# MLP down projection, segments 0 to 2: seven block products of sums for each pair of column tiles

## Chip, cores and metric

The kernel runs on one core of a Trainium2 chip. The metric is the device time of one execution in microseconds (us), the median of several runs. The profile is of one further execution.

## What is computed

A decoder trunk of two layers runs on 512 prompt positions and 64 sample positions, T = 576 columns together. Layer 0 mixes with attention and an S5 scan, layer 1 with a Mamba-2 SSD. After each mixer stands an MLP of width 4096 on a model width of 1024, and this is what the change touches:

```python
def _sq_relu_mlp(h, w_up, w_down):
    a = jax.nn.relu(h @ w_up)
    return (a * a) @ w_down
...
x = x + _rmsnorm(m, p['norm_mix_post'][i])
h = _rmsnorm(x, p['norm_mlp_pre'][i])
x = x + _rmsnorm(_sq_relu_mlp(h, p['w_mlp_up'][i], p['w_mlp_down'][i]), p['norm_mlp_post'][i])
```

All is float32. Each operand of a large product is split into a high and a low part (fp32r), and three matmuls, high by high, high by low and low by high, take the place of one.

## The kernel before

Activations lie transposed: features on the 128 partitions, the 576 columns in two halves of 288 (`hf` 0 and 1). A weight block `w` is 1024 input features by 128 output features, one DMA of 512 KB. `split_block` makes its parts `wh` (ScalarE copy, line 289) and `wl` (VectorE subtraction, line 304), each 128x1024 values, in a ring of NS = 9 buffers; the raw block has a ring of NW = 2.

`project3` goes over (tile, half) in the order of `rounds`. One such group is eight chunks of three matmuls (lines 318, 339, 340) of 128x128 by 288 columns, 24 in all, summed in one of three PSUM banks `mm`, and then read by the function `evac`. With `first` or `last` given to `rounds`, all tiles pass for half 0 and then all for half 1, so that all eight weight blocks must be held; out_proj_even and the last down projection do so (TAIL = 8), and so does the first up projection of a layer (LEAD = 8).

`mlp` runs four segments. In each, eight up tiles (16 groups) give 1024 of the 4096 hidden features: `up` takes relu times the norm's factor on VectorE (line 991), the square on ScalarE (line 286), and splits the result into `a2` (line 289 on ScalarE, line 347 on VectorE). Then the down projection (16 groups) multiplies this segment's eight chunks with `w_dn`; `down` copies the sums to `m` in segment 0 (ScalarE, line 289) and adds them to `m` in segments 1 to 3 (VectorE, line 1005). In segment 3 it also gathers the squares for the norm that follows (line 203 on GpSimd). So the down projections of segments 0 to 2 in two layers are 6 stages of 16 groups of 24 matmuls.

The order of instructions on every engine is that of a scheduler which plays the program through with estimated durations; each engine then works strictly in its order and waits on semaphores. Tiles of a ring wait until the earlier tile in the same buffer is no longer read. The SSD part (lines 1369, 1389) and the odd layer's out_proj (line 1198) are not touched by the change; their rows serve for durations.

Of the kernel before, what the change touches and what calls it, by code (L numbers as in the profile page):

```python
# [9 lines left out]
F32 = mybir.dt.float32  # L10
F32R = mybir.dt.float32r
ACTF = mybir.ActivationFunctionType
ALU = mybir.AluOpType
# [6 lines left out]
T = SEQ + TS  # L20
HALF = T // 2
HV = ((0, HALF), (HALF, T))
# [195 lines left out]
class _Kernel:  # L218
    def __init__(self, tc, a, ctx):
# [5 lines left out]
        self.n = self.blocks = self.turn = 0  # L225
        self.share = SHARE_EVEN
        self.groups, self.pins, self.last = 0, [], None


    def nm(self, s):  # L230
# [58 lines left out]
        return self.nc.scalar.activation(out, in_, ACTF.Identity, **kw)  # L289


    def split_block(self, src, ring=None, cuts=1):

        raw = self.block(src, (8, 128), ring, cuts)
        pool, bufs = self.wp
        hi = pool.tile([128, 8, 128], F32R, tag="wh", name=self.nm("wh"), bufs=bufs)
        lo = pool.tile([128, 8, 128], F32R, tag="wl", name=self.nm("wl"), bufs=bufs)
        self.blocks += 1
        eng = self.nc.gpsimd if self.share and self.blocks % self.share == 0 else self.nc.vector
        n = 8 // cuts  # L300
        for i in range(cuts):
            f = lambda t: t[:, i * n:i * n + n].rearrange("p a b -> p (a b)")
# [673 lines left out]

    def mlp(self, layer, h, r, mx, done):

        m = self.halves(self.mring)
        nc = self.nc  # L980
        sums = [_Squares(self, 8, SQ_M[hf]) for hf in range(2)]
        up_w, dn_w = self.a[f"w_up{layer}"], self.a[f"w_dn{layer}"]
        for seg in range(4):
            a2 = {}

            def up(i, hf, ps):
                sl = slice(*HV[hf])
                if hf == 0:
                    a2[i] = [mx.tile([128, T], F32R, tag="a2" + p, name=self.nm("a2"), bufs=NA2) for p in "hl"]
                t = mx.tile([128, HALF], F32, tag="a2t", name=self.nm("a2t"), bufs=3)  # L990
                nc.vector.scalar_tensor_tensor(t, ps, 0.0, r[hf], op0=ALU.max, op1=ALU.mult)  # L991
                self.act(t, t, ACTF.Square)
                self.split_into(a2[i][0][:, sl], a2[i][1][:, sl], t)

            first = 8 * seg
            mts = list(range(first, first + 8))
            self.share = 0 if seg else SHARE_LEAD
            self.project3(lambda i: up_w[i, 0], self.rounds(mts, first=0 if seg else LEAD), self.chunk(h), up)

            def down(i, hf, ps):  # L1000
                out = m[hf][:, i, :]
                if seg == 0:
                    self.copy_a(out, ps)
                else:
                    nc.vector.tensor_tensor(out, out, ps, ALU.add)  # L1005
                if seg == 3:
                    sums[hf].add(out)
                    if i == 7:
                        done(hf, m[hf], sums[hf])

            self.project3(lambda i: dn_w[i, seg], self.rounds(range(8), last=TAIL if seg == 3 else 0), lambda c, hf: [t[:, slice(*HV[hf])] for t in a2[first + c]], down)


    def odd(self, h, spill, done):
# [416 lines left out]
    def run(self):  # L1431
        nc, tc, a = self.nc, self.tc, self.a
        self.start()
        o = self.even()
# [39 lines left out]

        def mlp_pools(es):
            mx = es.enter_context(tc.tile_pool(name=self.nm("mx"), bufs=1, reuse_waits="tile"))
            self.wp = es.enter_context(tc.tile_pool(name=self.nm("mw"), bufs=1, reuse_waits="tile")), NS
            return mx

        h2 = []  # L1480
        with ExitStack() as es:
            mx = mlp_pools(es)
            self.ln_exp_table()
            self.out_proj_even(o, to_mlp(0))
            self.mlp(0, h, r, mx, to_odd)
        self.odd(h2, xd, to_mlp(1, (None, self.xring)))
# [20 lines left out]
SQ_X = ("p", "p")  # L1507
SQ_P = ("pv", "pv")
SQ_G = "pv"
NS = 9  # L1510
NSE = 2
NSO = 2
NHB = 4
# [20 lines left out]
PS_D = "t"  # L1534
GLU_Q = 1
PS_Y = "at"
NA2 = 9
TAIL = 8
NCV = 6
NT2 = 5  # L1540
# [42 lines left out]
```

## Time and profile before

| what | value |
|---|---|
| median of 3 runs | 1802.25 us (1798.43 to 1804.58) |
| profiled execution | 1804.89 us |
| its span, first to last instruction | 1803.1 us |
| mean granted TensorE clock | 0.961 |
| TensorE matmul busy | 1707.7 us (95%) |
| VectorE, ScalarE, GpSimd busy | 1010.7, 695.8, 401.9 us |

Busy shares are means over stages that differ. The two MLPs lie at about 390 to 800 us and 1380 to 1790 us; up and down stages take turns in them, some 51 us each. Matmuls overlap in the array, so a single one shows about 295 ns while one starts every 133 ns. A line number can be that of a helper that many callers use; the names of the tiles tell them apart. In the profile `project` is the PSUM bank of `project3`, `a` the split activations of `mlp`, `a2t` their unsplit form.

### The profile page before, as it was taken

The page shows a single profiled execution, that of the slowest core. Times are in us where ns is not written, and L with a number is a line of the kernel's source. Part 1 is how long each engine was busy: PE and PEld are TensorE (multiplying, and loading weights), DVE is VectorE, ACT ScalarE, POOL GpSimd, SP SyncE. Part 2 cuts the span into 40 slices and gives each one's busy share as a digit, 9 for nine tenths or more (in the row PEclk, how much of TensorE's full clock was granted, in tenths as well). Part 3 has the DMA queues.
Part 4 walks back from the last instruction along what each step waited for, and adds up shares of the span by engine and source line. Part 5 has one row for each costly group of instructions (what it writes and reads, how often), then busy time and mean ns, then how long its engine had stood idle before and what let it go on. Part 6 is the DMA issues. An engine that isn't in the chain of part 4 may idle for free. (4 is left out here: it accounts for less than half of the span.)

```text
span 1803.1 us, 31677 instructions
## 1 busy us (share of the span) xinstructions
PE 1707.7 (95%) x13007; PEld 1575.2 (87%) x13007; DVE 1010.7 (56%) x1789; ACT 695.8 (39%) x1306; POOL 401.9 (22%) x489
## 2 busy tenths in 40 slices
PE   9998999899999999998899899999977999999997
PEld 8975666799999999997789789898767999999997
DVE  8755435476243433357788757877768624343334
ACT  5233434465242322334325536335245524132331
POOL 3532100141000000134465434432343100000002
PEclk9998889899999999998799999999968999999999
DMA  8568553522222222222132141232513322222201
GB/s 279 100 241 288 190 198 140 170 94 94 83 82 83 83 84 87 77 66 85 47 132 85 48 163 55 96 129 73 174 40 125 109 87 85 83 83 83 83 24 53
DMA packets 81649, 197.41 MB, mean 109 GB/s; under 512 B 20352, under 2 KB 32000, under 8 KB 81504
## 3 DMA queue, kind: packets, MB, share of 16 engines
q1 hardware_dynamic: 57568, 174.72, 28.2%
q10 hardware_dynamic: 23936, 20.67, 3.9%
q8 instruction: 102, 1.67, 0.4%
q14 instruction: 43, 0.35, 0.1%
HBM read 176.92 MB, written 18.44 MB: 108 GB/s over the span
## 5 line engine op out<-in xcount | busy, mean ns | idle before, releaser
L318 PE MATMUL project<-h,wh 128*128 128x288 f32 x1808 | 547.0, 304 | 15.9 <-ACT raw L289 7.9
L339 PE MATMUL project<-h,wh 128*128 128x288 f32 x1808 | 546.4, 303 | 6.8 <-DVE h L395 6.5
L340 PE MATMUL project<-h,wl 128*128 128x288 f32 x1808 | 544.8, 302 | 2.5 <-DVE wl L304 2.5
L289 ACT ACTIVATE wh<-w 128x1024 fp32r<-128x1024 f32 (+1 forms) x215 | 225.4, 1050 | 458.0 <-PE project L339 347.7
L318 PEld LDWEIGHTS project<-h,wh 128*128 128x128 f32 x1808 | 348.1, 193 | 26.2 <-ACT raw L289 9.2
L339 PEld LDWEIGHTS project<-h,wh 128*128 128x128 f32 x1808 | 348.7, 193 | 15.8 <-DVE h L395 9.0
L340 PEld LDWEIGHTS project<-h,wl 128*128 128x128 f32 x1808 | 348.3, 193 | 9.2 <-issue 4.5
L304 DVE TENSOR_TENSOR wl<-w,wh 128x1024 fp32r<-128x1024 f32 (+1 forms) x196 | 243.9, 1247 | 188.9 <-ACT wh L289 187.3
L340 PE MATMUL project<-a,wl 128*128 128x288 f32 x1024 | 302.1, 295 | 0.0
L318 PE MATMUL project<-a,wh 128*128 128x288 f32 x1024 | 301.6, 295 | 0.0
L339 PE MATMUL project<-a,wh 128*128 128x288 f32 x1024 | 301.5, 294 | 0.0
L318 PEld LDWEIGHTS project<-a,wh 128*128 128x128 f32 x1024 | 192.1, 188 | 0.2
L340 PEld LDWEIGHTS project<-a,wl 128*128 128x128 f32 x1024 | 192.1, 188 | 0.1
L339 PEld LDWEIGHTS project<-a,wh 128*128 128x128 f32 x1024 | 192.1, 188 | 0.1
L203 POOL TENSOR_TENSOR nacc<-nacc,nsq 128x288 f32<-128x288 f32 x88 | 82.8, 942 | 485.9 <-ACT nsq L286 457.8
L1005 DVE TENSOR_TENSOR m<-m,project 128x288 f32<-128x288 f32 x96 | 43.5, 453 | 173.7 <-PE project L340 173.7
L304 POOL TENSOR_TENSOR wl<-w,wh 128x1024 fp32r<-128x1024 f32 x19 | 46.1, 2426 | 398.3 <-ACT wh L289 390.1
L991 DVE SCALAR_TENSOR_TENSOR a2t<-project,nht 128x288 f32<-128x288 f32 x128 | 58.2, 457 | 104.6 <-PE project L340 104.6
L286 ACT ACTIVATE a2t<-a2t 128x288 f32<-128x288 f32 x128 | 55.6, 435 | 113.5 <-DVE a2t L991 113.4
L347 DVE TENSOR_TENSOR a<-a2t,a 128x288 fp32r<-128x288 f32 x128 | 61.8, 486 | 53.7 <-ACT a L289 53.7
L1191 PE MATMUL out_proj<-x,wh 128*128 128x288 f32 x256 | 77.3, 304 | 3.0 <-DVE m L1198 2.6
L1045 DVE SCALAR_TENSOR_TENSOR cacc<-raw,cw,cacc 128x600 f32<-128x600 f32 x72 | 69.7, 968 | 14.1 <-POOL cacc L1043 13.1
(481 smaller groups left out, 2671.7 us busy)
## 6 DMA issues: line engine op xcount, KB each, us to landing
w<-in_w_up SPq DMA_DIRECT2D x64, 512.0 KB, 3.5
w<-in_w_dn SPq DMA_DIRECT2D x64, 512.0 KB, 3.5
w<-in_ck SPq DMA_DIRECT2D x40, 512.0 KB, 5.0
w<-in_cv SPq DMA_DIRECT2D x40, 512.0 KB, 6.0
w<-in_w_in_o SPq DMA_DIRECT2D x40, 512.0 KB, 3.5
w<-in_w_out_o SPq DMA_DIRECT2D x20, 512.0 KB, 3.5
hb<-in_h SPq DMA_DIRECT2D x32, 256.0 KB, 4.0
out_ssm_s<-hn ACTq DMA_DIRECT2D x32, 256.0 KB, 3.6
```

The costliest lines, as they stand in the source:

```text
L203: eng.tensor_tensor(self.acc[way], self.acc[way], sq, ALU.add)
L286: return self.nc.scalar.activation(out, in_, func, **kw)
L289: return self.nc.scalar.activation(out, in_, ACTF.Identity, **kw)
L304: eng.tensor_tensor(f(lo), f(raw), f(hi).bitcast(F32), ALU.subtract)
L318: self.nc.tensor.matmul(*args, **kw)
L339: self.nc.tensor.matmul(out, wh[:, c, :], xl, start=False, stop=False)
L340: self.nc.tensor.matmul(out, wl[:, c, :], xh, start=False, stop=(c == 7))
L347: self.nc.vector.tensor_tensor(lo, t, hi.bitcast(F32), ALU.subtract)
L991: nc.vector.scalar_tensor_tensor(t, ps, 0.0, r[hf], op0=ALU.max, op1=ALU.mult)
L1005: nc.vector.tensor_tensor(out, out, ps, ALU.add)
L1045: stt(acc, raw[:, k:k + 600], cw[:, 4 * m + k:4 * m + k + 1], acc, op0=ALU.mult, op1=ALU.add)
L1191: nc.tensor.matmul(out, wh[:, c, :], gh[:, k, :], start=(k == 0), stop=False)
```

## The change

For segments 0 to 2 the down projection takes output tiles in four pairs. In a pair the operands are seen as 2x2 blocks: output tiles by K halves (four blocks of 128 by 512, `a11` to `a22`, from two weight blocks), and K halves by column halves (four blocks of 512 by 288). Seven products of sums of blocks (the Winograd form of Strassen's scheme) take the place of eight products; one product is four chunks of three matmuls, 12 in all.

GpSimd makes the four sums of weight blocks (`s1` to `s4`, 128x512 each) and the sums of activations (`t1` to `t4`, four subtractions of 128x288 for each of four chunks in a segment); each sum is split again. Products go in the order of PAIR_STEPS. Products 1 and 2 share one PSUM sum, 6, 7 and 4 another, 5 and 3 a third: the bank is read after every product and the next product goes on adding to it. Product 1 goes to a new accumulator `e1`, the rest to the tiles of `m`; in the first segment the first reading of each accumulator is a ScalarE copy, all other readings are VectorE additions. In segment 3 GpSimd adds `e1` to the other three tiles of each pair (12 additions of 128x288 a layer). Up tiles run in the order 0, 4, 1, 5, 2, 6, 3, 7 in segments 0 to 2.

Buffers: NS goes from 9 to 5, `a2t` from 3 to 8 buffers (NC), the activation parts have one buffer each; where eight weight blocks must be held, the buffers of `t2` to `t4` serve as three more (`spare`).

```diff
--- before.py
+++ after.py
@@ -225,6 +225,7 @@
         self.n = self.blocks = self.turn = 0
         self.share = SHARE_EVEN
         self.groups, self.pins, self.last = 0, [], None
+        self.mx, self.spare = None, []
     def nm(self, s):
@@ -289,12 +290,19 @@
         return self.nc.scalar.activation(out, in_, ACTF.Identity, **kw)
+    def part_tiles(self):
+        if self.spare:
+            k = self.spare.pop(0)
+            return [self.mx.tile([128, 4 * HALF], F32R, tag=f"at{k}{p}", name=self.nm("w" + p), bufs=1)[:, :1024]
+                    .rearrange("p (a b) -> p a b", a=8) for p in "hl"]
+        pool, bufs = self.wp
+        return [pool.tile([128, 8, 128], F32R, tag="w" + p, name=self.nm("w" + p), bufs=bufs) for p in "hl"]
     def split_block(self, src, ring=None, cuts=1):
         raw = self.block(src, (8, 128), ring, cuts)
-        pool, bufs = self.wp
-        hi = pool.tile([128, 8, 128], F32R, tag="wh", name=self.nm("wh"), bufs=bufs)
-        lo = pool.tile([128, 8, 128], F32R, tag="wl", name=self.nm("wl"), bufs=bufs)
+        hi, lo = self.part_tiles()
         self.blocks += 1
         eng = self.nc.gpsimd if self.share and self.blocks % self.share == 0 else self.nc.vector
         n = 8 // cuts
@@ -976,39 +984,129 @@
     def mlp(self, layer, h, r, mx, done):
         m = self.halves(self.mring)
         nc = self.nc
         sums = [_Squares(self, 8, SQ_M[hf]) for hf in range(2)]
         up_w, dn_w = self.a[f"w_up{layer}"], self.a[f"w_dn{layer}"]
+        e1 = [mx.tile([128, HALF], F32, tag=f"e1{i}", name=self.nm("e1"), bufs=1) for i in range(4)]
         for seg in range(4):
-            a2 = {}
+            last = seg == 3
+            act = {k: [mx.tile([128, 4 * HALF], F32R, tag=f"a{k}{p}", name=self.nm(f"a{k}"), bufs=1)
+                       .rearrange("p (a b) -> p a b", a=4) for p in "hl"]
+                   for k in (("11", "21", "22", "t1") if last else ("11", "21", "22", "t1", "t2", "t3", "t4"))}
+            names = {(0, 0): "11", (1, 0): "21", (0, 1): "t1", (1, 1): "22"}
+            keep = {}
             def up(i, hf, ps):
-                sl = slice(*HV[hf])
-                if hf == 0:
-                    a2[i] = [mx.tile([128, T], F32R, tag="a2" + p, name=self.nm("a2"), bufs=NA2) for p in "hl"]
-                t = mx.tile([128, HALF], F32, tag="a2t", name=self.nm("a2t"), bufs=3)
+                kh, j = divmod(i % 8, 4)
+                t = m[0][:, i, :] if seg == 0 and hf == 0 else mx.tile([128, HALF], F32, tag="a2t", name=self.nm("a2t"), bufs=NC)
                 nc.vector.scalar_tensor_tensor(t, ps, 0.0, r[hf], op0=ALU.max, op1=ALU.mult)
                 self.act(t, t, ACTF.Square)
-                self.split_into(a2[i][0][:, sl], a2[i][1][:, sl], t)
-            first = 8 * seg
-            mts = list(range(first, first + 8))
+                keep[kh, hf, j] = t
+                part = lambda k: [p[:, j, :] for p in act[k]]
+                if last or (kh, hf) != (0, 1):
+                    self.split_into(*part(names[kh, hf]), t)
+                if not last and hf == 1:
+                    sub = lambda o, a, b: nc.gpsimd.tensor_tensor(o, a, b, ALU.subtract)
+                    if kh == 0:
+                        t1 = keep["t1", j] = mx.tile([128, HALF], F32, tag="a2t", name=self.nm("a2t"), bufs=NC)
+                        sub(t1, t, keep[0, 0, j])
+                        self.split_into(*part("t1"), t1)
+                    else:
+                        t1, b12, b21 = keep["t1", j], keep[0, 1, j], keep[1, 0, j]
+                        sub(t1, t, t1)
+                        self.split_into(*part("t2"), t1)
+                        sub(b12, t, b12)
+                        self.split_into(*part("t3"), b12)
+                        sub(b21, b21, t1)
+                        self.split_into(*part("t4"), b21)
+            mts = [8 * seg + i for i in ((0, 4, 1, 5, 2, 6, 3, 7) if not last else range(8))]
             self.share = 0 if seg else SHARE_LEAD
+            if seg == 0:
+                self.spare = [2, 3, 4]
             self.project3(lambda i: up_w[i, 0], self.rounds(mts, first=0 if seg else LEAD), self.chunk(h), up)
+            if not last:
+                self.down_pairs(lambda i: dn_w[i, seg], act, m, e1, seg == 0, mx)
+                continue
+            self.spare = [2, 3, 4]
+            for i in range(4):
+                for o in (m[0][:, 2 * i + 1, :], m[1][:, 2 * i, :], m[1][:, 2 * i + 1, :]):
+                    nc.gpsimd.tensor_tensor(o, o, e1[i], ALU.add)
             def down(i, hf, ps):
                 out = m[hf][:, i, :]
-                if seg == 0:
-                    self.copy_a(out, ps)
-                else:
-                    nc.vector.tensor_tensor(out, out, ps, ALU.add)
-                if seg == 3:
-                    sums[hf].add(out)
-                    if i == 7:
-                        done(hf, m[hf], sums[hf])
-            self.project3(lambda i: dn_w[i, seg], self.rounds(range(8), last=TAIL if seg == 3 else 0), lambda c, hf: [t[:, slice(*HV[hf])] for t in a2[first + c]], down)
+                nc.vector.tensor_tensor(out, out, ps, ALU.add)
+                sums[hf].add(out)
+                if i == 7:
+                    done(hf, m[hf], sums[hf])
+            self.project3(lambda i: dn_w[i, seg], self.rounds(range(8), last=TAIL),
+                          lambda c, hf: [p[:, c % 4, :] for p in act[names[c // 4, hf]]], down)
+    def pair_parts(self, src, i, mx):
+        nc = self.nc
+        raw = self.block(src(2 * i), (8, 128)), self.block(src(2 * i + 1), (8, 128), (mx, "w2", 2))
+        flat = lambda t, a: t[:, 4 * a:4 * a + 4, :].rearrange("p a b -> p (a b)")
+        a11, a12, a21, a22 = [flat(w, a) for w in raw for a in range(2)]
+        sums = [mx.tile([128, 8, 128], F32, tag="ws", name=self.nm("ws"), bufs=2) for _ in range(2)]
+        s1, s2, s4, s3 = [flat(w, a) for w in sums for a in range(2)]
+        out = {}
+        def split(key, pieces):
+            hi, lo = self.part_tiles()
+            for a, (k, t) in enumerate(zip(key, pieces)):
+                self.copy_a(flat(hi, a), t)
+                nc.vector.tensor_tensor(flat(lo, a), t, flat(hi, a).bitcast(F32), ALU.subtract)
+                out[k] = lambda c, hi=hi, lo=lo, a=a: (hi[:, 4 * a + c, :], lo[:, 4 * a + c, :])
+        op = lambda o, a, b, f: nc.gpsimd.tensor_tensor(o, a, b, f)
+        op(s1, a21, a22, ALU.add)
+        op(s2, s1, a11, ALU.subtract)
+        split((1, 2), (a11, a12))
+        split((5, 6), (s1, s2))
+        op(s4, a12, s2, ALU.subtract)
+        op(s3, a11, a21, ALU.subtract)
+        split((3, 7), (s4, s3))
+        split((4,), (a22,))
+        return out
+    def down_pairs(self, src, act, m, e1, first, mx):
+        nc = self.nc
+        right = {1: "11", 2: "21", 3: "22", 4: "t4", 5: "t1", 6: "t2", 7: "t3"}
+        bank_of = {1: "a", 2: "a", 6: "b", 7: "b", 4: "b", 5: "c", 3: "c"}
+        begin = 1, 6, 5
+        parts, banks, seen = {}, {}, set()
+        for i, p in PAIR_STEPS:
+            if i not in parts:
+                parts[i] = self.pair_parts(src, i, mx)
+            kind = bank_of[p]
+            if p in begin:
+                banks[i, kind] = (self.dacps if i % 2 else self.accps)("pair") if kind == "b" else self.mmps("pair")
+            ps = banks[i, kind][:, :HALF]
+            for c in range(4):
+                wh, wl = parts[i][p](c)
+                xh, xl = [t[:, c, :] for t in act[right[p]]]
+                go_on = dict(start=False, skip_group_check=p not in begin)
+                nc.tensor.matmul(ps, wh, xh, **(dict(start=True) if p in begin and c == 0 else go_on), stop=False)
+                nc.tensor.matmul(ps, wh, xl, **go_on, stop=False)
+                nc.tensor.matmul(ps, wl, xh, **go_on, stop=c == 3)
+            m11, m21, m12, m22 = [m[hf][:, 2 * i + k, :] for hf in range(2) for k in range(2)]
+            name, out = {1: (0, e1[i]), 2: (11, m11), 6: (12, m12), 7: (22, m22), 4: (21, m21), 5: (22, m22), 3: (12, m12)}[p]
+            if first and (i, name) not in seen:
+                seen.add((i, name))
+                self.copy_a(out, ps)
+            else:
+                nc.vector.tensor_tensor(out, out, ps, ALU.add)
     def odd(self, h, spill, done):
@@ -1474,6 +1572,7 @@
         def mlp_pools(es):
             mx = es.enter_context(tc.tile_pool(name=self.nm("mx"), bufs=1, reuse_waits="tile"))
+            self.mx = mx
             self.wp = es.enter_context(tc.tile_pool(name=self.nm("mw"), bufs=1, reuse_waits="tile")), NS
             return mx
@@ -1481,6 +1580,7 @@
         with ExitStack() as es:
             mx = mlp_pools(es)
             self.ln_exp_table()
+            self.spare = [2, 3, 4]
             self.out_proj_even(o, to_mlp(0))
             self.mlp(0, h, r, mx, to_odd)
         self.odd(h2, xd, to_mlp(1, (None, self.xring)))
@@ -1507,7 +1607,7 @@
 SQ_X = ("p", "p")
 SQ_P = ("pv", "pv")
 SQ_G = "pv"
-NS = 9
+NS = 5
 NSE = 2
 NSO = 2
 NHB = 4
@@ -1534,7 +1634,11 @@
 PS_D = "t"
 GLU_Q = 1
 PS_Y = "at"
-NA2 = 9
+NC = 8
+PAIR_STEPS = [(0, 1), (0, 5), (0, 2), (0, 6), (0, 3), (0, 7)]
+for _i in range(1, 4):
+    PAIR_STEPS += [(_i, 1), (_i - 1, 4)] if _i == 1 else [(_i, 1)]
+    PAIR_STEPS += [(_i, _p) for _p in (6, 2, 7, 5, 4, 3)]
 TAIL = 8
 NCV = 6
 NT2 = 5
```

## Rows read from the trace of the kernel before

**Rows 1.** The page, part 1: engine, busy time (share of the span), instructions.

```profile
PE 1707.7 (95%) x13007; PEld 1575.2 (87%) x13007; DVE 1010.7 (56%) x1789; ACT 695.8 (39%) x1306; POOL 401.9 (22%) x489
```

**Rows 2.** Busy time by stretch; columns as in the first line.

```profile
core 0: us, PE busy (x) PEld busy (x) DVE busy (x) ACT busy (x) POOL busy (x), PEclk, DMA share, GB/s
...
446.10:497.20 51.10, 51.10 (x388) 51.10 (x387) 9.91 (x9) 14.15 (x24) 0.00 (x0) 1.00 0.25 84
497.20:548.30 51.10, 51.10 (x385) 51.10 (x385) 23.66 (x41) 21.82 (x40) 0.00 (x0) 1.00 0.24 83
548.30:599.40 51.10, 51.10 (x388) 51.10 (x387) 17.30 (x25) 8.48 (x8) 0.00 (x0) 1.00 0.24 84
...
341.00:391.00 50.00, 47.34 (x327) 46.31 (x327) 29.52 (x35) 29.37 (x57) 17.24 (x17) 0.93 0.35 117
1340.00:1410.00 70.00, 57.91 (x375) 55.01 (x374) 56.17 (x86) 40.64 (x81) 33.68 (x32) 0.88 0.33 113
```

**Rows 3.** Timeline of TensorE in a down stage: start us, duration us, line.

```profile
659.56 0.29 PE L340 MATMUL project<-a,wl 128*128 128x288 f32 x1
659.69 0.29 PE L318 MATMUL project<-a,wh 128*128 128x288 f32 x1
659.82 0.29 PE L339 MATMUL project<-a,wh 128*128 128x288 f32 x1
```

**Rows 4.** Timeline of VectorE there; idle before and releaser in brackets.

```profile
656.73 0.46 DVE L1005 TENSOR_TENSOR m<-m,project 128x288 f32<-128x288 f32 x1 [1.01 <-PE project L340]
659.89 0.46 DVE L1005 TENSOR_TENSOR m<-m,project 128x288 f32<-128x288 f32 x1 [2.70 <-PE project L340]
```

**Rows 5.** Groups by line and form: count; busy us, mean ns; idle before, releasers.

```profile
L340 PE MATMUL project<-a,wl 128*128 128x288 f32 x1024 | 302.1, 295 | 0.0
...
L991 DVE SCALAR_TENSOR_TENSOR a2t<-project,nht 128x288 f32<-128x288 f32 x128 | 58.2, 457 | 104.6 <-PE project L340 104.6
L289 ACT ACTIVATE a<-a2t 128x288 fp32r<-128x288 f32 x128 | 56.6, 443 | 3.7
L286 ACT ACTIVATE a2t<-a2t 128x288 f32<-128x288 f32 x128 | 55.6, 435 | 113.5 <-DVE a2t L991 113.4
...
L286 ACT ACTIVATE mt<-mt 128x512 f32<-128x512 f32 x32 | 20.2, 630 | 24.2 <-DVE mt L1387 23.9
...
L289 ACT ACTIVATE m<-project 128x288 f32<-128x288 f32 x48 | 19.2, 401 | 38.3 <-PE project L340 38.3
```

**Rows 6.** Single lines: ns min/median/max, first and last start us, forms.

```profile
L318 PE MATMUL project<-a,wh x384: 288/295/297, 442.8 to 697.5; 128*128 128x288 f32 x192
...
L1005 DVE TENSOR_TENSOR m<-m,project x96: 439/455/456, 548.3 to 1789.8; 128x288 f32<-128x288 f32 x96
L1198 DVE TENSOR_TENSOR m<-m,out_proj x48: 436/447/456, 1193.9 to 1370.3; 128x288 f32<-128x288 f32 x48
L347 DVE TENSOR_TENSOR a<-a2t,a x128: 445/453/1546, 395.4 to 1739.9; 128x288 fp32r<-128x288 f32 x128
L304 DVE TENSOR_TENSOR wl<-w,wh x55: 1217/1226/1227, 424.8 to 744.8; 128x1024 fp32r<-128x1024 f32 x55
L1389 DVE TENSOR_TENSOR mt<-mt,cb x24: 674/693/2172, 951.3 to 1316.5; 128x512 f32<-128x512 f32 x24
L1369 POOL TENSOR_TENSOR hn<-hb,et x32: 1056/1064/2191, 924.0 to 1288.2; 128x512 f32<-128x512 f32 x32
L203 POOL TENSOR_TENSOR nacc<-nacc,nsq x88: 792/837/1792, 8.0 to 1787.7; 128x288 f32<-128x288 f32 x88
```

**Rows 7.** Timelines of VectorE and GpSimd in the odd layer, 1087 to 1091 us.

```profile
1087.65 2.40 POOL L304 TENSOR_TENSOR wl<-w,wh 128x1024 fp32r<-128x1024 f32 x1 [1.52 <-ACT wh L289]
...
1088.42 2.17 DVE L1389 TENSOR_TENSOR mt<-mt,cb 128x512 f32<-128x512 f32 x1 [0.91 <-ACT mt L286]
```

**Rows 8.** Waits of TensorE around each mixer's end: total us, times, longest.

```profile
PE project L318 <- ACT wh L289: 3.6, 1, 3.6
...
PE project L339 <- DVE h L395: 4.4, 1, 4.4
```

## Prediction

> **What bounds the kernel now.** I read the busy times first: TensorE is busy 95% of the span, every other engine 56% or less [rows 1]. A mean says nothing of one stage, so next came the busy time by stretch: in the down stages of segments 0 and 1 and the up stage between them TensorE is busy 51.1 of 51.1 us at the full granted clock, VectorE 9.9 to 23.7 us, ScalarE 8.5 to 21.8, GpSimd not at all [rows 2]. No wait ends last there: the number of matmuls sets the time. What one costs is not its duration (295 ns, overlapped [rows 5]) but the step between starts, 0.13 us in the timeline [rows 3]. More exactly: from the first down matmul of line 318 in segment 0, at 442.8, to the last in segment 2, at 697.5 [rows 6], lie three down and two up stages less the last two matmuls, so 5 x 384 - 3 = 1917 steps in 254.7 us, **132.9 ns** each. Only at the ends of the mixers is TensorE not full: 47.3 of 50 us and 57.9 of 70, at a clock of 0.93 and 0.88 [rows 2].
>
> **What is removed.** The 3072 matmuls of all down stages (three lines, 1024 each [rows 5]) hold 2304 in segments 0 to 2, that is 24 pairs of 96. A pair now takes 7 x 4 x 3 = 84. So 24 x 12 = 288 matmuls go, at 132.9 ns: **38.3 us**. They are on the path, as the full stretches show, so without new waits the gain is whole. A pair shrinks from 12.76 us to 11.16, a product lasts 12 x 0.1329 = 1.59 us.
>
> **What is added in a down stage, per pair.** VectorE made two low parts of 1024 and read four banks: 2 x 1.226 + 4 x 0.455 = 4.3 us [rows 6]. It now makes seven low parts of 512 and reads seven banks: 7 x 0.693 + 7 x 0.455 = 8.0 us of 11.16. (The 512-wide subtraction has no row of its own; the 512-wide product of line 1389 stands for it, 0.693; a line through 0.453 at 288 and 1.226 at 1024 gives the same.) ScalarE makes seven high parts, 7 x 0.630 = 4.4 us, and in the first segment also five readings at 0.401 [rows 5], so there VectorE has only two readings. GpSimd makes four sums of 512: nearest is line 1369, 1.064 [rows 6], so 4.3 us. Transfers are the same blocks as before. None of this reaches 11.16 us; beside TensorE it costs nothing by itself.
>
> **The new wait.** Product 2 adds to the bank of product 1 and so must wait until that has been read; likewise 7 behind 6, 4 behind 7, 3 behind 5. One other product always stands between. A read starts at once behind the last matmul today: that started at 659.56, the read at 659.89 [rows 3, 4], 0.33 later; it takes 0.455, and I estimate 0.04 for the way back, as long as the way there. So the bank is free 0.83 us after the last start, and wanted 0.13 + 1.59 = 1.73 us after it. **The slack is 0.9 us**: VectorE may be that late before TensorE stops. Behind one unhindered low part (0.69) a read is still in time; behind two (1.39) it costs up to 0.5.
>
> **Where VectorE is late.** Its low parts and GpSimd's sums both read two operands in SBUF, and the trace shows what happens when they meet: GpSimd started a subtraction at 1087.65 for 2.40 us; VectorE's 512-wide product, started at 1088.42, took 2.17 and ended 0.54 behind it [rows 7], as if it had stood still until GpSimd was through. The medians and maxima say the same, 0.693 against 2.172, and 0.453 against 1.546 [rows 6]. The reads are not hit: they have one operand in PSUM, and line 1198, in a part of the kernel where GpSimd works, never exceeds 0.456 [rows 6]. So a low part behind a sum takes up to 0.69 + 1.06 = 1.75, and a read queued behind it costs TensorE up to 0.85 us.
>
> Laid out by hand over the seven slots: buffers of the next pair come free after products 2, 5, 4 and 3, and the low parts made then bunch at the end of a pair, five of them (3.5 us) and three readings (1.4) between the end of product 5 and that of the next product 1, three slots of 1.59 (4.8 us). GpSimd's sums may start when the low parts of the pair before are done, in the same stretch. With no collision all is just in time; with two sums standing in the way (2.1 us) the read behind product 1 is late by 2.2, less 0.9 of slack. Against that, the order is chosen with readings in it, sums also run early, and the last pair of a segment has none. I take 0.4 us per pair, between 0 and 1.3: **24 x 0.4 = 9.6 us lost, bounds 0 and 31**.
>
> The Trainium skill (GPSIMD Engine Reference, section Key points) states that GpSimd shares its SBUF interfaces with VectorE and contends with VectorE instructions that have two SBUF inputs. The trace agrees, with 2.172 us against 0.693 [rows 6]; it speaks against putting the sums on GpSimd. Were every sum to stop VectorE by that rule, rival 2's time would hold in place of the forecast's.
>
> **Up stages.** Per segment 12 more splits (ScalarE 12 x 0.443, VectorE 12 x 0.453: about 5.4 us each) and 16 subtractions on GpSimd (16 x 0.837 = 13.4) [rows 5, 6]. VectorE goes from 23.7 to 29 of 51 us [rows 2], and three banks give it two groups (6.4 us) of room. Nothing. The last sums come late: behind the last up group `t2` needs 0.457 + 0.435 + 0.837 + 0.443 + 0.453 = 2.6 us; its low part is wanted in the fourth product, over 4.8 us later; `t3` and `t4` have more. Covered by over 2 us; if queues eat that, 1 us per segment. In segment 3 GpSimd's twelve additions (10 us) lie in an up stage. Nothing.
>
> **Fewer buffers.** 5 + 3 for the weights where eight must be held, where there were nine. The next stage's first block is prepared one group (3.2 us) later. Each block has eight groups (25 us) between its buffer's release and its first use, but VectorE and ScalarE carry the norms there, and TensorE has already waited 3.6 us for a high part and 4.4 for `h` [rows 8]. The three spare buffers also lie at other addresses, which the mixers may release later. Unknown, 4 us lost or 2 won at each of two places, taken at **1 us each, 2 in all**.
>
> **Sum.** 38.3 - 9.6 - 2 = 26.7 us. The profiled execution took 1804.9, so 1778.2 for one like it; it is 2.6 above the median of 1802.25, and **on that the forecast is 1776 us**, its own range 1767 to 1786.
>
> **Rivals.**
> 1. *The gain is whole.* The readings always make it: 1802 - 38 = 1764 us. For it: VectorE idle 30%, reads that PSUM keeps out of the collisions. Against: the bunching. Chance 0.26.
> 2. *VectorE becomes the bound.* Each GpSimd sum stops it for its whole length: 8.0 + 4.3 = 12.3 us per pair instead of 11.16 in the 18 pairs with sums behind them, 20 us lost, plus the 2: 1786 us, up to 1797 with more waiting at the mixers' ends. Against: half of the collisions should hit GpSimd, which has time. Chance 0.12.
> 3. *The readings stand behind stopped low parts, slower.* All 96 continuing products wait s. The gain is gone at s = 38.3 / 96 = 0.40 us, and slower beyond that; at 0.6 (of the 0.85 above) the time is 1802 + 58 - 38 = 1822 us. Gaps of that kind may also lower the clock, as in the stretches at 0.93 and 0.88 [rows 2]. Against: segment 0 reads mostly by ScalarE, and not all four reads of a pair lie in the bunch. Chance 0.16, and 0.07 for ending near no change.
> The forecast keeps 0.39.
>
> **How the numbers follow.** Measurements of this kernel tell about 0.3% (5.4 us) from no change. Faster by more: 0.39 + 0.26 + 0.12 = 0.77, less 0.01 for its tail: 0.76; same 0.08; slower 0.16. Below 1762 only if costs are below nothing (0.03); of the slower case two thirds lie above 1812. So the range is 1762 to 1812.
>
> **What will show it.** Down stages of 44.7 us with TensorE full would be rival 1; 46 to 47 us, with waits of products on VectorE's readings (tile `m` or `e1`), the forecast; VectorE busy nearly throughout, rival 2; waits of 0.4 us or more on all readings, rival 3. Low parts of 512 should show 0.69 as median and 1.2 to 1.8 where GpSimd works; readings 0.455 throughout. The forecast is wrong if TensorE waits for weight parts (`wl`) or `t` splits rather than for readings, or if the first MLP groups start several us later against the mixer's end.

## The result, and the profile after

The changed kernel takes 1774.25 us (median; 1769.1 to 1776.06) against 1802.34 us of the kernel before: a ratio of 0.984, 95% interval 0.982 to 0.987. In a second comparison on another chip it was 0.985 (0.982 to 0.987). The forecast was 1776 us. The profiled execution took 1776.06 us, its span is 1773.9 us. The gain of 28.1 us is the forecast's 26.7 almost to the point; but the losses that stand behind it are not where the prediction put them.

The page of the changed kernel, part 1 (compare [rows 1]):

```profile
PE 1665.1 (94%) x12719; PEld 1532.1 (86%) x12719; DVE 1190.5 (67%) x2045; ACT 770.9 (43%) x1506; POOL 670.4 (38%) x705
```

TensorE has 288 matmuls fewer (13007 less 12719), as counted. VectorE works 180 us more, GpSimd 268 us more. Busy time by stretch, to be held against [rows 2]; the first row is segment 0's down stage, then up and down stages take turns:

```profile
core 0: us, PE busy (x) PEld busy (x) DVE busy (x) ACT busy (x) POOL busy (x), PEclk, DMA share, GB/s
444.70:494.50 49.80, 48.74 (x360) 47.67 (x359) 31.85 (x43) 26.07 (x54) 19.54 (x16) 1.00 0.31 97
494.50:542.90 48.40, 48.40 (x366) 48.40 (x365) 34.07 (x52) 24.24 (x51) 24.45 (x20) 1.00 0.26 87
542.90:591.40 48.50, 48.50 (x367) 48.50 (x366) 36.51 (x59) 18.97 (x32) 16.85 (x12) 1.00 0.29 89
```

From segment 1 on TensorE is full at the full clock, though VectorE's load in a down stage has doubled, from 17.3 to 36.5 us. Only segment 0 has a hole. The cuts follow the scheduler's order, in which the last product and the next up group overlap, so up and down stages are best taken together. Single lines (columns as in [rows 6]) give the marks: the first down matmul of segment 3 in the kernel before,

```profile
L318 PE MATMUL project<-a,wh x128: 290/295/506, 749.0 to 801.0; 128*128 128x288 f32 x128
```

and in the changed kernel the first matmul of a pair:

```profile
L1100 PE MATMUL pair<-a,wh x144: 288/295/398, 444.7 to 686.9; 128*128 128x288 f32 x144
```

Segment 3, which the change leaves as plain groups, begins there at 734.6:

```profile
L326 PE MATMUL project<-a,wh x96: 288/295/507, 734.6 to 786.8; 128*128 128x288 f32 x96
```

From the first down matmul of segment 0 to that of segment 3 the kernel before takes 749.0 - 442.8 [rows 6] = 306.2 us, the changed one 734.6 - 444.7 = 289.9. The other layer gives the same two numbers. So the MLPs win 2 x 16.3 = **32.7 us of 38.3**. By segment (up stage of the next included): 98.2, 95.9 and 95.9 us instead of 102.1 each. A whole gain would be 102.1 - 6.4 = 95.7. Segments 1 and 2 have it to 0.2 us; segment 0 lacks 2.3 us more per layer. The rest of the span is 1190.7 us before and 1194.2 after, but it scatters: the kernel before with one buffer less shows 1177.1 there, and all profiles of this study lie between that and 1205.1, while the MLP stages of the changed kernel are the same to 0.1 us in both layers of both its profiles. That is why the stages, and not the whole, carry the readings below.

What each kernel takes from the first down matmul of segment 0 to that of segment 3, and its time against the kernel before on the same chip:

| kernel | layer 0, layer 1 (us) | ratio, 95% interval |
|---|---|---|
| before | 306.2, 306.2 | 1 |
| changed | 289.9, 289.9 | 0.984 (0.982 to 0.987) |
| product 1 twice | 308.7, 308.7 | 1.008 (1.006 to 1.009) |
| no weight sums | 287.6, 287.6 | 0.980 (0.979 to 0.982) |
| written order kept | 300.1, 300.2 | 0.998 (0.995 to 1.000) |
| side by side, order kept | 331.3, 331.3 | 1.031 (1.028 to 1.034) |
| side by side, free | 290.6, 290.6 | 0.987 (0.984 to 0.989) |
| LEAD = 7 | 287.9, 290.3 | 0.986 (0.983 to 0.988) |
| LEAD = 6 | 287.6, 288.7 | 0.989 (0.986 to 0.993) |
| pairs in segments 1 and 2 | 294.2, 294.2 | 0.991 (0.989 to 0.994) |
| sums on VectorE | 288.8, 288.8 | 0.982 (0.980 to 0.985) |
| every bank read twice | 295.9, 297.4 | 0.991 (0.989 to 0.993) |
| before, eight buffers | 306.2, 306.2 | 0.998 (0.997 to 1.000) |

### The profile page after: what moved, and what is told of

Its sections match the earlier page's. It is cut to its first block, busy times and chain, and to the rows that moved or that the text cites. A ratio compares the mean times of both kernels' runs of the same rounds, so it can differ in the third digit from the quotient of the medians.

```text
span 1773.9 us, 31866 instructions
## 1 busy us (share of the span) xinstructions
PE 1665.1 (94%) x12719; PEld 1532.1 (86%) x12719; DVE 1190.5 (67%) x2045; ACT 770.9 (43%) x1506; POOL 670.4 (38%) x705
## 4 chain that ended last, share of the span: by engine, by line
PE 38%; DVE 7%; ACT 2%; POOL 2%; issue 1%; DMA 1%; DVEq 0%; ACTq 0%; POOLq 0%
PE project L326 7%; PE project L347 7%; PE project L348 7%; PE pair L1100 2%; PE pair L1101 2%; PE pair L1102 2%; PE out_proj L1291 2%; PE out_proj L1289 2%; PE out_proj L1290 2%; PE ssd_group L1499 1%; DVE m L381 1%; DVE wl L312 1%; PE ssd_group L1420 1%; PE ssd_group L1454 1%; DVE cacc L1143 1%
## 5 line engine op out<-in xcount | busy, mean ns | idle before, releaser
L312 DVE TENSOR_TENSOR wl<-w,wh 128x1024 fp32r<-128x1024 f32 (+1 forms) x148 | 189.3, 1285 | 104.1 <-ACT wh L290 101.6
L1014 POOL TENSOR_TENSOR a2t<-a2t,a2t 128x288 f32<-128x288 f32 x80 | 83.9, 1065 | 172.6 <-ACT a2t L287 167.8
L1101 PE MATMUL pair<-at,wh 128*128 128x288 f32 x384 | 112.8, 296 | 1.1 <-DVE at L355 1.1
L1102 PE MATMUL pair<-at,wl 128*128 128x288 f32 x384 | 111.7, 295 | 0.0
L1100 PE MATMUL pair<-at,wh 128*128 128x288 f32 x384 | 111.3, 295 | 0.0
L355 DVE TENSOR_TENSOR at<-a2t,at 128x288 fp32r<-128x288 f32 x96 | 65.8, 689 | 34.6 <-ACT at L290 34.6
L1067 DVE TENSOR_TENSOR wl<-ws,wh 128x512 fp32r<-128x512 f32 x96 | 83.0, 903 | 4.3 <-ACT wh L290 3.5
L1100 PE MATMUL pair<-a,wh 128*128 128x288 f32 x288 | 85.2, 296 | 0.6 <-DVE a2t L1006 0.6
L1101 PE MATMUL pair<-a,wh 128*128 128x288 f32 x288 | 84.8, 295 | 0.0
L1102 PE MATMUL pair<-a,wl 128*128 128x288 f32 x288 | 84.4, 295 | 0.5 <-DVE wl L1067 0.5
L1289 PE MATMUL out_proj<-x,wh 128*128 128x288 f32 x256 | 77.4, 304 | 3.0 <-DVE m L1296 2.5
L1143 DVE SCALAR_TENSOR_TENSOR cacc<-raw,cw,cacc 128x600 f32<-128x600 f32 x72 | 69.7, 968 | 13.5 <-POOL cacc L1141 12.5
L1291 PE MATMUL out_proj<-x,wl 128*128 128x288 f32 x256 | 76.9, 304 | 0.7 <-POOL wl L312 0.4
L1290 PE MATMUL out_proj<-x,wh 128*128 128x288 f32 x256 | 76.9, 301 | 0.0
```

The lines of the kernel that those rows point to most:

```text
L312: eng.tensor_tensor(f(lo), f(raw), f(hi).bitcast(F32), ALU.subtract)
L1100: nc.tensor.matmul(ps, wh, xh, **(dict(start=True) if p in begin and c == 0 else go_on), stop=False)
L1101: nc.tensor.matmul(ps, wh, xl, **go_on, stop=False)
L1102: nc.tensor.matmul(ps, wl, xh, **go_on, stop=c == 3)
L1143: stt(acc, raw[:, k:k + 600], cw[:, 4 * m + k:4 * m + k + 1], acc, op0=ALU.mult, op1=ALU.add)
L1289: nc.tensor.matmul(out, wh[:, c, :], gh[:, k, :], start=(k == 0), stop=False)
```

## The experiments

**What the matmuls alone are worth.** Product 1 is computed twice:

```diff
-            for c in range(4):
+            for c in (range(8) if p == 1 else range(4)):
+                c = c % 4
```

> Product 1 of every pair is computed twice (the second pass begins the sum anew), so a pair has 96 matmuls again, as before the change, with everything else of the change kept. Theory (the number of matmuls alone sets the down stages): 24 x 12 x 132.9 ns = 38.3 us more than the changed kernel's 1774, so 1812, some 10 us above the kernel before; these 10 us are what the change costs beside its matmuls. Rival (VectorE or GpSimd sets the pace of a pair, so that TensorE has room): less than 25 us more, under 1800.

1812.76 us. The stages take 2 x (308.7 - 289.9) = 37.6 us more: 131 ns for each of 288 matmuls, against the 132.9 of the sum. (Segment 0's hole is 0.5 us smaller per layer here, which takes a little off.) In segment 1's down stage TensorE is full again, with VectorE about as busy as in the changed kernel; nothing else sets the pace there:

```profile
541.00:592.20 51.20, 51.20 (x386) 51.20 (x386) 35.58 (x55) 18.48 (x31) 15.69 (x12) 1.00 0.24 79
```

The kernel stands 14 us above the one before, not 10; 5.0 of them lie in the MLP stages, the others in the parts that scatter.

**Do GpSimd's sums cost anything?** The four additions of `pair_parts` are left out:

```diff
-        op(s1, a21, a22, ALU.add)
-        op(s2, s1, a11, ALU.subtract)
         split((1, 2), (a11, a12))
-        split((5, 6), (s1, s2))
-        op(s4, a12, s2, ALU.subtract)
-        op(s3, a11, a21, ALU.subtract)
-        split((3, 7), (s4, s3))
+        split((5, 6), (a21, a12))
+        split((3, 7), (a22, a11))
         split((4,), (a22,))
```

> The four sums of weight blocks on GpSimd are left out (products 5, 6, 3 and 7 take plain blocks instead), the splits stay; so the output is not the reference's. Theory (VectorE's low parts do collide with GpSimd's sums, but TensorE does not wait for it): 1774, within 3 us of the changed kernel; low parts of 512 at 0.69 us throughout. Rival (the term of 9.6 us in the prediction, readings late behind stopped low parts): 5 to 10 us faster, 1764 to 1769.

1763.01 us, and the rival's number, not the theory's; but the kernel before, too, is 3.6 us faster on this chip (1798.73), so the stages say it better. In them the sums cost 2 x 2.3 = 4.6 us, and all of it in segment 0 (95.9 us instead of 98.2; segments 1 and 2 are unchanged). So the theory holds for four of the six down stages. The rival's reason, late readings, does not hold in the other two either: the waits there are mostly for parts, as the section on the hole shows. The collisions themselves are there. Low parts of 512 (line 1067), weight sums (line 1070) and readings (line 1109) in the changed kernel:

```profile
L1067 DVE TENSOR_TENSOR wl<-ws,wh x96: 677/685/1778, 436.2 to 1644.7; 128x512 fp32r<-128x512 f32 x96
L1067 DVE TENSOR_TENSOR wl<-w,wh x72: 678/693/1786, 432.6 to 1650.1; 128x512 fp32r<-128x512 f32 x72
...
L1070 POOL TENSOR_TENSOR ws<-w x24: 1288/1298/2253, 338.4 to 1633.1; 128x512 f32<-128x512 f32 x24
...
L1109 DVE TENSOR_TENSOR m<-m,pair x112: 439/453/455, 460.2 to 1662.1; 128x288 f32<-128x288 f32 x112
```

A low part takes 0.69 us as median and up to 1.79, as forecast; readings stay at 0.455. Timelines of VectorE and then GpSimd in segment 2's down stage show it at work (`e` is the accumulator `e1`, `pair` the PSUM sum of a product; the GpSimd row at 660.56 is one of the additions of `e1`, which the scheduler has moved forward):

```profile
659.46 2.90 DVE L1067 TENSOR_TENSOR wl<-ws,wh 128x512 fp32r<-128x512 f32 x2
662.28 0.44 DVE L1109 TENSOR_TENSOR e<-e,pair 128x288 f32<-128x288 f32 x1
662.85 0.46 DVE L1109 TENSOR_TENSOR m<-m,pair 128x288 f32<-128x288 f32 x1
...
664.98 2.51 DVE L1067 TENSOR_TENSOR wl<-w,wh 128x512 fp32r<-128x512 f32 x2
667.41 0.81 DVE L1109 TENSOR_TENSOR m<-m,pair 128x288 f32<-128x288 f32 x2
```

```profile
659.31 1.29 POOL L1070 TENSOR_TENSOR ws<-w 128x512 f32<-128x512 f32 x1 [2.25 <-DVE wl L1067]
660.56 1.25 POOL L1041 TENSOR_TENSOR m<-m,e 128x288 f32<-128x288 f32 x1
661.78 1.74 POOL L1070 TENSOR_TENSOR ws<-ws,w 128x512 f32<-128x512 f32 x1
```

Two low parts take 2.90 us instead of 1.39, and readings pile up behind low parts, two in a row at 667.41. Yet TensorE does not stop anywhere in this stage. Why not is the question of the next two runs.

**Who keeps the readings out of the way?** The matmuls of the products are kept in the written order:

```diff
-                nc.tensor.matmul(ps, wh, xl, **go_on, stop=False)
+                keep = self.tc.keep_in_program_order
+                keep(nc.tensor.matmul(ps, wh, xl, **go_on, stop=False))
```

(and so for all three matmuls of a chunk).

> The matmuls of the products keep the written order of PAIR_STEPS on TensorE, twelve of a product in one piece; the scheduler, which in the changed kernel puts 2 to 9 matmuls of other products where a reading is due, may not move them. Theory (that filling is why no reading is waited for): waits on readings appear, as the prediction's slack of 0.9 us gives them: 0.4 us a pair, 5 to 15 us in all, 1779 to 1789. Rival (one product in between is enough by itself): 1774, within 3 us.

1794.95 us, ratio 0.998: nearly the whole gain is gone, more than the theory said. The built instruction lists show what was taken away; the trace of TensorE has pieces of the same lengths. Below, each entry is one PSUM sum (numbered) and how many matmuls it gets in one piece on TensorE; first the changed kernel, then the one with the written order, both in segment 1:

```
1003:12 1004:12 1005:9 1018:5 1003:12 1005:3 1004:12 1018:7 1020:2 1005:12 1019:12 1020:5
1003:12 1004:12 1003:12 1005:12 1004:12 1005:12 1018:12 1005:12 1019:12 1018:12 1019:12 1020:12
```

In the changed kernel the scheduler cut products into pieces and put pieces of the next pair between. So at most places more than one product lies between a sum's two turns (in this list 21 to 29 matmuls instead of 12), and up groups stand between the last ones of a stage. With the written order, waits for readings (`e`, `m`) show in segments 1 and 2, and these segments take 2 x 5.3 = 10.6 us more than in the changed kernel: the readings cost what the theory said, 5 to 15 us. The waits of TensorE there, 540 to 750 us (the changed kernel has none in that stretch; lines are one number higher in this kernel):

```profile
PE pair L1101 <- DVE e L1110: 2.7, 2, 1.7
PE pair L1101 <- DVE m L1110: 0.8, 3, 0.3
```

The other 2 x 4.9 us are lost in segment 0, and not at readings. Stretches of 4 us there, columns as above:

```profile
444.00:448.00 4.00, 1.69 (x13) 1.46 (x11) 4.00 (x6) 1.67 (x5) 3.66 (x4) 1.00 0.38 135
448.00:452.00 4.00, 2.41 (x8) 2.09 (x9) 2.65 (x6) 1.85 (x6) 2.19 (x3) 0.58 0.43 130
452.00:456.00 4.00, 4.00 (x21) 4.00 (x20) 2.12 (x4) 1.89 (x4) 0.29 (x2) 0.56 0.00 1
456.00:460.00 4.00, 4.00 (x32) 3.95 (x31) 3.16 (x4) 2.01 (x4) 3.29 (x3) 1.00 0.01 2
```

TensorE first waits for an activation part (3.1 us idle in the view of waits) and is then granted the lower of its two levels, 1.2 GHz, for most of 448 to 456 us: the row from 452 counts 21 matmuls in 4 us, the one behind it 32.

**And with no product in between?** Products of one bank stand side by side, and that order is kept:

```diff
-PAIR_STEPS = [(0, 1), (0, 5), (0, 2), (0, 6), (0, 3), (0, 7)]
...
+PAIR_STEPS = [(_i, _p) for _i in range(4) for _p in (1, 2, 5, 3, 6, 7, 4)]
```

> Products that share a bank stand directly one behind the other (1 2, 5 3, 6 7 4), and this order is kept on TensorE. The bank is free 0.83 us after the start of a product's last matmul and wanted 0.13 us after it: each of 96 continuing products waits 0.70 us, more where VectorE is late. Theory: 96 x 0.70 = 67 us and up to 110 us more, 1841 to 1884, the whole gain lost. Rival (readings in the middle of a sum cost little): under 1800.

1855.23 us. The stages take 2 x 41.4 = 82.8 us more than in the changed kernel: 0.86 us for each of 96 continuing products. In the trace 78 of the 96 wait; the other 18, in the last pair of each stage, have matmuls of an up group in front of them. The shortest of the 78 waits costs 0.76 us and the middle one 0.87, against 0.70 worked out from a reading's way there and back; the long ones, up to 4.5, stand behind readings that came late. So the prediction's price of one such wait is about right, if some 0.06 low.

The same written order, with the scheduler free:

> Products that share a bank are written one behind the other, as in the run with the kept order, but the scheduler may move their matmuls. In the built order it puts products of the next pair and pieces of 2 to 10 matmuls between them; only in the last pair of a down stage do two or three products of one bank stand in a row (24 and 28 matmuls in one piece). Theory (the scheduler's order, not the written one, decides): about two unfilled waits of 0.7 us in each of 6 stages, 4 to 12 us over the changed kernel. Rival: like the kept order, 60 us or more.

1779.63 us, ratio 0.987, and 290.6 us in the stages: 0.7 us per layer behind the changed kernel, all in segment 0. The waits that the theory expected at the ends of stages don't come, since the free up groups fill those too. The theory's point holds more strongly than it was stated: between these two written orders it made 1.4 us in the stages.

**The hole in segment 0.** In the changed kernel no wait of TensorE between 444 and 495 us is for the reading of a product. It waits for a part of an activation sum (`at`), for the reading of the last up group (`a2t`, line 1006), whose bank a product takes next, and for a weight part (`wl`):

```profile
PE pair L1101 <- DVE at L355: 0.5, 2, 0.3
PE pair L1100 <- DVE a2t L1006: 0.3, 1, 0.3
PE pair L1102 <- DVE wl L1067: 0.2, 1, 0.2
```

(The idle time sums to 1.0 us; counted by the steps between starts, the loss is 2.3.) Busy time just before the down stage, and VectorE's row behind the last up group:

```profile
432.00:444.70 12.70, 12.70 (x97) 12.70 (x96) 12.39 (x17) 7.96 (x17) 10.14 (x9) 1.00 0.13 41
```

```profile
446.09 2.53 DVE L355 TENSOR_TENSOR at<-a2t,at 128x288 fp32r<-128x288 f32 x2
448.55 0.45 DVE L1006 SCALAR_TENSOR_TENSOR a2t<-project,nht 128x288 f32<-128x288 f32 x1
```

The last up group ended by 444.7 and is read at 448.55, 3.9 us later: VectorE is busy 12.39 of 12.7 us, GpSimd 10.14, and they stop each other. The share alone does not tell: without weight sums, where there is no hole, VectorE is busy 12.19 of the 12.7 us ahead of the first down matmul (at 437.0 there), but 20 of its instructions fall into them instead of 17, and it reads the last up group 1.1 us behind that matmul:

```profile
438.10 0.45 DVE L1006 SCALAR_TENSOR_TENSOR a2t<-project,nht 128x288 f32<-128x288 f32 x1
```

Segment 0 passes half 1 of all tiles in one go, so all `t` sums fall in half of the up stage, together with the first pair's weight sums. One or two tiles less in that pass:

```diff
-LEAD = 8
+LEAD = 7
```

> In segment 0 seven up tiles instead of eight pass by halves, the eighth does both halves at the end. In the changed kernel TensorE loses 2.3 us per layer in the first pair of segment 0, behind activation parts that VectorE makes late, as the pass over half 1 has all their work in half the time. Theory: the last chunk's t1 is made two groups sooner, the loss falls to about 1 us per layer, 2 to 3 us faster than the changed kernel (1771 to 1772 where that takes 1774). Rival: half 1 of h is wanted one group (3.2 us) sooner and TensorE waits for that instead, no change or up to 4 us slower.

1772.15 us, ratio 0.986: no change. Layer 0 wins 2.0 us in its stages, layer 1 nothing (98.6 us in segment 0), where TensorE now waits for the reading of an up group instead (1.7 us in the view of waits). With LEAD = 6:

> The same with six tiles by halves. Theory: the loss in the first pair of segment 0 is gone, 4 to 5 us faster than the changed kernel. Rival: half 1 of h is wanted two groups (6.4 us) sooner, TensorE waits for it at the start of both layers' MLPs, up to 8 us slower.

1781.02 us, ratio 0.989. The hole in segment 0 is nearly gone (95.9 and 97.0 us), as the theory said, but the kernel is not faster, as the rival said. In layer 1 TensorE now waits for half 1's activations (in the buffer `x` there), a row that the changed kernel does not have:

```profile
PE project L326 <- ACT x L290: 2.7, 1, 2.7
```

The rest of the loss is in the parts that scatter, and stays open.

**What segment 0 is worth.** Pairs in segments 1 and 2 alone:

```diff
-            last = seg == 3
+            last = seg in (0, 3)
...
+            if seg == 0:
+                self.project3(lambda i: dn_w[i, 0], self.rounds(range(8)), x, lambda i, hf, ps: self.copy_a(m[hf][:, i, :], ps))
+                continue
```

> Pairs of seven products in segments 1 and 2 alone; segment 0 does its plain down projection into m, buffers stay as changed. Theory (each stage of pairs is worth the matmuls that it saves, less the waits of segment 0): up and down stage of segment 0 take 102.1 us again instead of 98.2, so 2 x 3.9 = 8 us slower than the changed kernel, 1782 where that takes 1774. Rival (segment 0 costs elsewhere what it gives, at the start of the MLP): within 3 us of the changed kernel.

1782.35 us, ratio 0.991. The stages take 4.3 us more per layer, 8.6 in all, near the theory's 8. (The lines left out give segment 1 the first reading by copy, of `e1` alone.) Segment 0's pairs are worth having, hole and all.

**The sums on the other engine.**

```diff
-        op = lambda o, a, b, f: nc.gpsimd.tensor_tensor(o, a, b, f)
+        op = lambda o, a, b, f: nc.vector.tensor_tensor(o, a, b, f)
```

> The four sums of weight blocks go from GpSimd to VectorE: 4 x 0.69 us more per pair there, 10.8 of 11.16 us, and no collisions in the down stages. Theory (a low part that meets a sum stands still for about as long as VectorE would need for the sum itself): within 4 us of the changed kernel, either way. Rival (VectorE becomes the bound, readings late behind its own sums): 8 to 25 us slower.

1767.07 us, ratio 0.982. The stages win 1.1 us per layer, in segment 0. VectorE is busier for it, but by less than the sums take. From the first down matmul of segment 0 to that of segment 3 in layer 0, columns as above, first the changed kernel, then this one, then the one without weight sums:

```profile
444.70:734.60 289.90, 288.84 (x2162) 287.77 (x2161) 198.68 (x301) 134.73 (x255) 112.28 (x91) 1.00 0.29 95
439.40:728.20 288.80, 288.50 (x2162) 287.73 (x2161) 205.22 (x343) 134.97 (x254) 52.10 (x48) 1.00 0.30 96
437.00:724.60 287.60, 287.60 (x2163) 287.60 (x2162) 177.02 (x298) 133.99 (x252) 51.62 (x48) 1.00 0.29 96
```

Without the sums VectorE works 177.0 us. Sums on GpSimd cost it 21.7 us more in stopped low parts and splits, sums of its own 28.2. So the theory is near: three quarters of what GpSimd relieves VectorE of is lost again in stops. That half of the hole goes although VectorE has more to do is not explained by its load; GpSimd, which makes the `t` sums too, has less to do, but whether that is the reason was not tried. This version beats the kernel before; against the changed kernel the intervals overlap (0.980 to 0.985, 0.982 to 0.987), so only the 2.2 us in the stages are shown.

**How much VectorE has to spare.** Every bank is read a second time:

```diff
+            nc.vector.scalar_tensor_tensor(out, ps, 0.0, out, op0=ALU.mult, op1=ALU.add)
```

> VectorE reads every bank a second time (adding zero times the sum), 0.455 us more for each of the seven readings of a pair, so 3.2 us per pair: VectorE comes to 11.2 of 11.16 us before collisions, and the slack of a reading falls from 0.9 to 0.45 us. Theory (VectorE had some 12 us to spare in a down stage, which these 28 x 0.455 = 12.7 us use up): waits appear, 5 to 30 us over the changed kernel. Rival (readings and VectorE's load don't matter to TensorE): within 4 us of the changed kernel.

1784.09 us, ratio 0.991, some two fifths of the changed kernel's gain lost; 13.5 us in the stages. Segment 1's down stage and the waits from 534 to 732 us:

```profile
537.80:586.80 49.00, 47.67 (x356) 47.26 (x356) 44.36 (x83) 18.31 (x32) 16.36 (x12) 1.00 0.29 93
```

```profile
PE pair L1100 <- DVE m L1110: 3.2, 2, 1.8
```

So waits on readings do come at a VectorE load of 44.4 of 49 us, with each bank freed 0.455 us later. At 36.5 of 48.5 there are none. Which of the two, the load or the later bank, brings the waits was not told apart, nor where between the two loads they begin.

**Fewer buffers.** The kernel before, with one weight buffer less:

```diff
-NS = 9
+NS = 8
```

> The kernel before with eight weight buffers instead of nine, the number that the changed kernel has where eight blocks must be held (5 and 3). Theory (the prediction's term for fewer buffers): 0 to 3 us slower than the kernel before, ratio 1.000 to 1.002. Rival (the mixers' ends wait for each buffer): 5 us or more, ratio over 1.003.

Ratio 0.998 (0.997 to 1.000): not slower. The ninth buffer was worth nothing to the kernel before. That the three spare buffers lie at other addresses was not tried alone.

The changed kernel once more, on another chip:

> The changed kernel once more, beside the other kernels of this call on the same chip: 0.984 of the kernel before.

0.985, and stages of 289.9 us again.

## Why the prediction was right, and where it was not

**The gain of 38.3 us** is right: 37.6 us come back when the twelve matmuls of a pair are put back.

**The new wait, 9.6 us**, is more than what the MLPs lose in all (5.6 us), and for a wrong reason. The step that failed is "One other product always stands between". The prediction took the written PAIR_STEPS for TensorE's order, although the kernel's order comes from a scheduler that may move single matmuls; it does, and in segments 1 and 2 no reading is ever waited for. By the prediction's own signs its mechanism was wrong: down stages with TensorE full stood for rival 1, and waits for `wl` or `t` splits rather than for readings for a wrong forecast; segments 1 and 2 show the one, segment 0 the other. The price of a wait was sound (0.76 us at least where nothing stands between, 0.70 reckoned). For the order on which it was argued the term was of the right kind and a little small: kept in the written order, segments 1 and 2 lose 10.6 us at readings, 0.66 for each of 16 pairs where 0.4 was taken. The stages lose 20.4 us in all, within the bound of 31, but the rest of it, in segment 0, is a late activation part and the lower clock behind it, which the prediction did not have. So in segments 1 and 2 rival 1 is what happened, and with the order fixed it would have been near "no change".

**Collisions** are as forecast in size (1.79 us at most, 1.75 reckoned) and kind; readings keep their 0.455 us. A sum was put too low, at 1.06 us: none of the weight sums took less than 1.28. With that length the same reckoning, 0.69 + 1.29, gives 1.98, so the meeting of 1.75 and 1.79 is in part luck. The stops go both ways, as the prediction has it against rival 2: a sum behind a low part takes 1.74 us in the timeline above, and up to 2.25 in the row. Rival 2, VectorE as the bound, does not come true: 36.5 of 48.5 us with all its stops. The Trainium skill (GPSIMD Engine Reference, section Key points) says that GpSimd and VectorE contend in SBUF when VectorE reads two operands there. The runs agree: low parts, with two operands in SBUF, take up to 1.79 us instead of 0.69, readings, with one in PSUM, never more than 0.455, and the sums on GpSimd cost VectorE 21.7 us per layer.

**Up stages, "nothing"**, is wrong for segment 0. 29 of 51 us is a mean over the stage, and there the sums fall in one half of it, with VectorE at 12.39 of 12.7 us. The chain of 2.6 us behind the last up group was reckoned from a reading at once, and that reading came 3.9 us late; "if queues eat that, 1 us per segment" was the right thought, with 2.3 us in segment 0 and nothing in the others. The whole loss that the MLPs show beyond the step between starts (132.9 ns before, about 133.2 after; 1.0 us in all) lies here: 4.6 us, and it goes when the weight sums go, and most of it goes with LEAD = 6.

**Fewer buffers, 2 us**: the count costs nothing in the kernel before. What is lost outside the MLP stages, 32.7 - 28.1 = 4.6 us, can't be told from the scatter of those parts; one piece repeats, the stretch from the first down matmul of segment 3 in layer 1 to the end, 64.9 us before and 65.1 to 66.0 in all kernels with the change.

So the total was met by luck: what was put down as lost (9.6 at readings and 2 at buffers) comes out like what was lost (4.6 in a hole that was not foreseen, 1.0 by a slower step, and 4.6 outside the stages). The chances gave the forecast's mechanism 0.39; rival 1, at 1764 us, is closer to it in mechanism for four of the six down stages, though not in time.

## What to carry to other kernels

Where the bound engine is full, count its instructions and multiply by the step between starts; put them back in a run to see that the count is right. For waits inside a dependent chain, read the order that was built, not the one that was written: the same products took 20 us longer here when the scheduler could not move them. And look for the half of a stage in which the extra work falls, since a mean over the stage hides it. When work moves to another engine, count what both do from the same mark to the same mark: the engine that was relieved can lose most of it again in stops.

## What the runs showed of the hardware

Where a VectorE instruction with two SBUF operands and a GpSimd one met here, one stood still until the other was through: two low parts took 2.90 us instead of 1.39, and a sum 1.74 instead of 1.29. Readings of products, with one operand in PSUM, were never longer than 0.455 us in the changed kernel. So moving the weight sums of 128x512 to GpSimd relieved VectorE of little: from mark to mark in a layer it was busy 198.7 us with them on GpSimd, 205.2 with them on itself, and 177.0 without them. And a stop of a few us cost more than its own length: in the kernel with the written order 3.1 us of waiting, and 0.8 soon after, were followed by matmuls that started every 0.24 us instead of 0.133, at the lower granted clock, until 455.5 us; the shorter holes of the changed kernel left the clock at 1.00.
